# A mixture of experts in plain fp32 on parts of the matmul array, with one of three programs per expert chosen by its token count

## The chip, the core and the metric

The kernel runs on one core of a Trainium2 chip. A core has a matmul engine (PE; its weight loads are a row of their own, PEld), two engines for elementwise work (DVE, ACT), a general one (POOL) and a sequencer that issues most transfers here (SP). PE multiplies a stationary operand, which is loaded into its 128 by 128 array first (up to 128 rows, the contraction, by up to 128 columns, which become output partitions), with a moving operand that streams through. A matmul whose stationary operand has 64 or 32 columns takes a half or a quarter of the array's columns; it writes 64 or 32 of the 128 partitions of a PSUM bank (128 partitions by 512 fp32 numbers). Weights come from HBM through 16 transfer (DMA) engines. The metric is device time in microseconds (us), lower is better.

## What is computed

Two blocks over 256 tokens of width 1024. Each has a mixer (pooling, convolution, an RWKV recurrence) and a feed-forward part; the first block's is dense, the second's a mixture of eight experts of which each token takes two. The change is in that mixture:

```python
def moe_swiglu(h, router, w_gate, w_up, w_down):
    logits = (xf @ router)
    top_val, top_idx = lax.top_k(logits, TOP_K)          # TOP_K = 2
    gates = jax.nn.softmax(top_val, axis=-1)
    ...                                                   # tokens sorted by expert
    # for each expert e, on its own tokens x:
    #   y = (silu(x @ w_gate[e]) * (x @ w_up[e])) @ w_down[e]
    # and y, times the token's gate, is added to the token's row
```

A weight matrix has 1024 by 3584 numbers, three to an expert, eight experts: 352 MB in fp32, each read once. How many of the 512 token places each expert gets depends on the inputs. Evaluating the reference's routing on its inputs gives, for experts 0 to 7: 58, 77, 58, 62, 58, 73, 50, 76.

## The kernel before

The program is written out in the order in which each engine runs it. Mixer and dense part of the first block, then the mixer of the second, take the first 528 us or so; then come the routing (`route`, `pick`, `places`, `gates`: rank the logits, number the tokens of each expert) and the experts (`run_experts`).

An expert is worked off in 7 chunks of 512 hidden columns. For a chunk, `gate_up` multiplies the expert's tokens (up to 128 of them, gathered by a matmul with a one-hot matrix `ge` into `mx`, transposed, so that the tokens are the stationary columns) with 1024 by 512 numbers of the gate and as many of the up weights; ACT takes silu of the first product, DVE multiplies by the second (`msl`); `hidden` transposes that by four PE transposes (`mtp`); `down`, one chunk behind, multiplies it with 512 by 1024 numbers of the down weights and accumulates in two PSUM banks (`ya`) over the seven chunks. After an expert, `evac` takes `ya` out, scaled by the gates, and `scatter` puts the rows back to their tokens by a matmul with `gT` and adds them to the residual `h`.

All of these products are made from two parts of each operand. ACT rounds a weight to the shorter fp32r format (`wh`), DVE takes the rest (`wl`), the activations are split likewise (`mx`, `mhhl` hold both parts), and each product is three matmuls, high by high, high by low, low by high:

```python
mm(pg[a], xh[:, k, :], wh[:, kk, :], k == 0, False)
mm(pg[a], xh[:, k, :], wl[:, kk, :], False, False)
mm(pg[a], xl[:, k, :], wh[:, kk, :], False, k == KT - 1)
```

Weights come in units of 1 MB (128 partitions by 2048 numbers), six units to a chunk. `stream` holds 15 raw units; a unit's buffer is free again as soon as ACT and DVE have split it (three pairs of split buffers). If an expert had more than 128 tokens, a second pass under `tc.If(rv > P)` at the end would take the rest; the register `rv` is loaded from the greatest count there, on all engines, and the branch jumps over the second pass. After it, `finish` norms `h` and writes it out.

Of the kernel before, what the change touches and what calls it, by code (L numbers as in the profile page):

```python
# [18 lines left out]
P = 128  # L19
# [16 lines left out]
def kernel(  # L36
# [56 lines left out]
    def mm(o, lhsT, rhs, start, stop):  # L93
        nc.tensor.matmul(o, lhsT, rhs, start=start, stop=stop)  # L94

# [351 lines left out]
    def mixer(l, N, pend, nxt, open_next):  # L447
# [32 lines left out]
        v_ = vfirst if l == 0 else kp.tile([P, 4, T], F32, name=f"v{l}")  # L480
# [705 lines left out]

        return nxw, lambda q, halves=(0, 1): add_h(q, [wo[q, n] for n in range(2)], halves), tidy
# [118 lines left out]
    def route(R, hT, cmp, rt, ones, tie):  # L1306
# [55 lines left out]
        def count():  # L1362
            cps = mm_bank("cps")
            for q in range(2):
                mm(cps[:, :NE], ones, sel[:, q, :], q == 0, q == 1)
            cnt = small("cnt", [P, 1])
            vec.tensor_reduce(cnt, cps[:, :NE], axis=AX.X, op=OP.max)
            vec.tensor_copy(small("cnti", [P, 1], I32), cnt)

        return tr, logits, pick, places, gates, count  # L1370
# [4 lines left out]
    LAST = ((0, 512, 0, 2), (0, 512, 2, 4), (512, 768, 0, 4), (768, 1024, 0, 4))  # L1375
    FINE = 2
    HALVES = ((0, 512), (512, 1024))

    def expert_units():
        seq = [(e, c) for e in range(NE) for c in range(NCH)]  # L1380
        units = []

        def gate_up(e, c, nk=4):
            for nm, src in (("g", moe_w_gate[0, e]), ("u", moe_w_up[0, e])):
                for k in range(0, KT, nk):
                    units.append((src[k * P:(k + nk) * P, c * 512:(c + 1) * 512]
                                  .rearrange("(k p) n -> p k n", p=P), (nk, 512), f"m{nm}{e}{c}{k}"))

        def down(e, c, nj=2):
            for j in range(0, 4, nj):  # L1390
                r0 = c * 512 + j * P
                units.append((moe_w_down[0, e][r0:r0 + nj * P, :].rearrange("(k p) n -> p k n", p=P),
                              (nj, D), f"md{e}{c}{j}"))

        def last_down(e, c):
            for a, b, k0, k1 in LAST:
                r0 = c * 512
                units.append((moe_w_down[0, e][r0 + k0 * P:r0 + k1 * P, a:b].rearrange("(k p) n -> p k n", p=P),
                              (k1 - k0, b - a), f"ml{a}{k0}"))

        for i, s in enumerate(seq):
            fine = i >= len(seq) - FINE
            gate_up(*s, 2 if fine else 4)
            if i:
                down(*seq[i - 1], 1 if fine else 2)
        last_down(*seq[-1])
        return units

    def moe(W, R, pend, tidy, prep):
        rstd = R.rstd  # L1410
        st = ExitStack()
        mo = st.enter_context(tc.tile_pool(name="mo", bufs=1, reuse_waits="tile"))
        sx = st.enter_context(tc.tile_pool(name="sx", bufs=1, reuse_waits="tile"))
        m2 = st.enter_context(tc.tile_pool(name="m2", bufs=1, reuse_waits="tile"))
        spare = st.enter_context(tc.tile_pool(name="spare", bufs=1, reuse_waits="tile"))
        mx = [st.enter_context(tc.tile_pool(name=f"mx{i}", bufs=1, reuse_waits="tile")) for i in range(2)]
        sb, sa, sc = [st.enter_context(tc.tile_pool(name=f"s{i}", bufs=1, reuse_waits="tile")) for i in "bac"]
        W.pairs.extend(((sa, "h", sa, "l"), (sx, "h", sx, "l"), (sb, "h", sc, "l")))

        pend(0)  # L1420
        W.split(lambda *a: low(nc.gpsimd, *a, 0, 2048))
        low1, low2 = [], []
        W.split(lambda *a: low1.extend(a))
        low(vec, *low1, 0, 1024)
        W.after = lambda: (tidy(), W.open_raw(st, {"y": (m3, "big"), "x": (mx[1], "mx")}, (spare,)))
        m3 = st.enter_context(tc.tile_pool(name="m3", bufs=1, reuse_waits="tile"))
        hT = m3.tile([P, 2, KT, P], F32, name="hT", tag="big")
        tr, logits, pick, places, gates, count = route(R, hT, m2.tile([P, 2, T], F32, name="cmp", tag="msl"), *prep)
        hn = mo.tile([P, 2, D], F32, name="hn")

        def make_hn(q, half):
            ns = slice(half * 512, (half + 1) * 512)
            vec.scalar_tensor_tensor(hn[:, q, ns], h[:, q, ns], rstd[q], g2b[:, ns], op0=OP.mult, op1=OP.mult)

# [6 lines left out]
        W.split(lambda *a: low2.extend(a))  # L1441
# [4 lines left out]
        low(nc.gpsimd, *low2, 0, 2048)  # L1446
# [3 lines left out]
        pos = R.t["pos"]  # L1450

        def onehot(e, base):
            g = m2.tile([P, 2, P], F32, name="ge", tag="ge")
            for q in range(2):
                vec.tensor_scalar(g[:, q, :], iota_f, float(base), pos[:, q, e:e + 1], op0=OP.add, op1=OP.is_equal)
            return g

        def weigh(e, g):
            for q in range(2):
                vec.tensor_scalar(g[:, q, :], g[:, q, :], R.t["gate"][:, q, e:e + 1], None, op0=OP.mult)  # L1460
# [12 lines left out]
        def gather(e, g, idx, xh, xl, k4, between):  # L1473
# [5 lines left out]
            for f in between:  # L1479
                f()  # L1480
# [212 lines left out]
```

## Time and profile before

| | us |
|---|---|
| median of 3 runs (1569.64 to 1571.14) | 1570.03 |
| the profiled execution, its own time | 1567.63 |
| its span, first to last instruction | 1565.8 |
| first expert matmul to last (552.5 to 1549.3 in the trace) | 996.8 |

Times within the trace count from the span's start. An instruction's duration holds its way through the engine's pipeline, and matmuls overlap: what a matmul costs in a series is the distance from its start to the next one's, which a merged row of the timeline gives as its length less the last duration, over the count less one. One plain fp32 matmul of the program is two passes, so two records, each with its weight load; an fp32r matmul is one, and so is a transpose. "PEclk" is the granted share of PE's clock, 1.00 for 2.4 GHz and 0.50 for 1.2 GHz.

### The profile page before, as it was taken

The page shows a single profiled execution, that of the slowest core. Times are in us where ns is not written, and L with a number is a line of the kernel's source. Part 1 is how long each engine was busy: PE and PEld are TensorE (multiplying, and loading weights), DVE is VectorE, ACT ScalarE, POOL GpSimd, SP SyncE. Part 2 cuts the span into 40 slices and gives each one's busy share as a digit, 9 for nine tenths or more (in the row PEclk, how much of TensorE's full clock was granted, in tenths as well). Part 3 has the DMA queues.
Part 4 walks back from the last instruction along what each step waited for, and adds up shares of the span by engine and source line. Part 5 has one row for each costly group of instructions (what it writes and reads, how often), then busy time and mean ns, then how long its engine had stood idle before and what let it go on. Part 6 is the DMA issues. An engine that isn't in the chain of part 4 may idle for free. (4 is left out here: it accounts for less than half of the span.)

```text
span 1565.8 us, 25264 instructions
## 1 busy us (share of the span) xinstructions
PE 1519.3 (97%) x10388; PEld 1293.3 (83%) x10388; DVE 1279.8 (82%) x1381; ACT 976.6 (62%) x937; POOL 71.9 (5%) x90
## 2 busy tenths in 40 slices
PE   8999999999999899999999999999999999999996
PEld 7888899998988688888888888888888888888885
DVE  8997754556988778898888889889889889888986
ACT  6443644345533476776776777677677677677765
POOL 3201300000110300000000000000000000000000
PEclk9999999999999899999999999999999999999998
DMA  6416265524525688999999999999999999999872
GB/s 193 149 44 229 75 212 171 191 74 130 153 69 174 241 333 312 355 360 344 354 361 348 337 376 346 338 367 357 330 373 353 343 356 358 344 353 361 291 242 99
DMA packets 202965, 422.64 MB, mean 270 GB/s; under 512 B 8624, under 2 KB 53048, under 8 KB 202840
## 3 DMA queue, kind: packets, MB, share of 16 engines
q1 hardware_dynamic: 201880, 419.10, 75.5%
q8 instruction: 83, 1.36, 0.4%
q0 software_dynamic: 672, 1.31, 0.3%
q10 hardware_dynamic: 288, 0.52, 0.1%
q14 instruction: 42, 0.34, 0.1%
HBM read 419.86 MB, written 1.05 MB: 269 GB/s over the span
## 5 line engine op out<-in xcount | busy, mean ns | idle before, releaser
L148 DVE TENSOR_TENSOR wl_mu<-mu,wh_mu 128x2048 fp32r<-128x2048 f32 (+1 forms) x115 | 255.0, 2217 | 48.4 <-ACT wh_mu L144 47.6
L94 PE MATMUL m0a<-wh_mg,mx 128*128 128x512 f32 x896 | 294.1, 398 | 0.0
L94 PE MATMUL m1a<-wh_mu,mx 128*128 128x512 f32 x896 | 292.1, 395 | 0.0
L148 DVE TENSOR_TENSOR wl_md<-md,wh_md 128x2048 fp32r<-128x2048 f32 (+1 forms) x114 | 252.0, 2217 | 42.3 <-ACT wh_md L144 41.8
L94 PE MATMUL ya<-wh_md,mhhl 128*128 128x512 f32 x880 | 285.6, 395 | 0.0
L148 DVE TENSOR_TENSOR wl_mg<-mg,wh_mg 128x2048 fp32r<-128x2048 f32 (+1 forms) x114 | 251.8, 2215 | 21.2 <-ACT wh_mg L144 20.6
L144 ACT ACTIVATE wh_mg<-mg 128x2048 fp32r<-128x2048 f32 (+1 forms) x116 | 215.5, 1860 | 74.5 <-PE ya L94 41.6
L144 ACT ACTIVATE wh_md<-md 128x2048 fp32r<-128x2048 f32 (+1 forms) x114 | 211.9, 1858 | 64.1 <-PE m0a L94 32.8
L144 ACT ACTIVATE wh_mu<-mu 128x2048 fp32r<-128x2048 f32 (+1 forms) x116 | 215.2, 1855 | 23.0 <-PE m0a L94 21.9
L94 PEld LDWEIGHTS m1a<-wh_mu,mx 128*128 128x128 f32 x896 | 168.3, 188 | 36.9
L94 PEld LDWEIGHTS ya<-wh_md,mhhl 128*128 128x128 f32 x880 | 165.0, 187 | 40.0
L94 PEld LDWEIGHTS m0a<-wh_mg,mx 128*128 128x128 f32 x896 | 168.4, 188 | 35.6
L94 PE MATMUL m1a<-wl_mu,mx 128*128 128x512 f32 x448 | 175.9, 393 | 0.0
L94 PE MATMUL m0a<-wl_mg,mx 128*128 128x512 f32 x448 | 175.7, 392 | 0.0
L94 PE MATMUL ya<-wl_md,mhhl 128*128 128x512 f32 x440 | 173.9, 395 | 0.0
L94 PEld LDWEIGHTS ya<-wl_md,mhhl 128*128 128x128 f32 x440 | 82.5, 187 | 20.4 <-DVE wl_md L148 0.2
L94 PEld LDWEIGHTS m1a<-wl_mu,mx 128*128 128x128 f32 x448 | 84.2, 188 | 17.7
L94 PEld LDWEIGHTS m0a<-wl_mg,mx 128*128 128x128 f32 x448 | 84.3, 188 | 17.0 <-DVE wl_mg L148 0.6
L1528 ACT ACTIVATE mhhl<-mtpa 128x512 fp32r<-128x512 f32 x55 | 33.0, 600 | 71.8 <-PE mtpa L97 71.8
L94 PE MATMUL fps<-xhf,wl_fu 128*128 128x256 f32 x176 | 49.9, 284 | 0.0
L94 PE MATMUL fps<-xhf,wh_fg 128*128 128x256 f32 x176 | 49.9, 284 | 0.0
L94 PE MATMUL fps<-xhf,wh_fu 128*128 128x256 f32 x176 | 49.8, 283 | 0.0
(431 smaller groups left out, 2545.3 us busy)
## 6 DMA issues: line engine op xcount, KB each, us to landing
mg<-in_moe_w_gate_dram SPq DMA_DIRECT2D x108, 1024.0 KB
mu<-in_moe_w_up_dram SPq DMA_DIRECT2D x108, 1024.0 KB
md<-in_moe_w_down_dram SPq DMA_DIRECT2D x106, 1024.0 KB
fg<-in_ffn_w_gate_dram SPq DMA_DIRECT2D x11, 1024.0 KB
fu<-in_ffn_w_up_dram SPq DMA_DIRECT2D x11, 1024.0 KB
fd<-in_ffn_w_down_dram SPq DMA_DIRECT2D x11, 1024.0 KB
wo<-in_w_out_dram SPq DMA_DIRECT2D x16, 512.0 KB
wik<-in_w_in_dram SPq DMA_DIRECT2D x8, 512.0 KB
```

The source lines that it names most:

```text
L94: nc.tensor.matmul(o, lhsT, rhs, start=start, stop=stop)
L144: act(wh[:, :n], t[:, :n], AF.Copy)
L148: vec.tensor_tensor(wl[:, :n], t[:, :n], wh.bitcast(F32)[:, :n], op=OP.subtract)
L1528: act(hh, tp, AF.Copy)
```

## The change

The split is gone: weights and activations stay fp32, and PE multiplies them as they are. The tokens of an expert are laid out in up to three groups. The first 64 are the stationary operand of matmuls on a half of the array: in `half`, half `s` of the array takes 256 of the chunk's 512 weight columns, so that the two halves work on the same tokens and different columns. Tokens 64 to 95, and 96 to 127, are stationary on a quarter (32 columns), and the four quarters take 128 weight columns each. `down` does the same with 512 and 256 columns. Results of all groups share one bank: 256 columns of it for the first group, 128 for each of the others.

Each expert is written three times, with two, one or no group of 32 (`n`). From the counts, DVE works out a number 0, 1 or 2 per expert (more than 96 tokens, 65 to 96, up to 64); PE, ACT, DVE and SP load all eight numbers into registers and branch by them at each expert (`tc.Switch`), with a prefetch hint for the next expert in the fifth chunk. Of the counts above, experts 1, 5 and 7 run with `n` = 1 and the other five with `n` = 0.

The ring of raw units has 16 places (7 in space that the mixer gave up, as before, and 9 more); a unit's place is free when PE has used it. `scatter` multiplies out of fp32 too: it gives each token two one-hot rows (`gT`, five layers of it, weighted), and runs on 64 rows at a time. The counting is moved ahead of the experts. The closing of the program, the mixers and the dense part stay.

```diff
+    def mma(o, lhsT, rhs, start=False):
+        nc.tensor.matmul(o, lhsT, rhs, start=start, stop=True, skip_group_check=True)
...
+    class Feed:
...
+        def send(self):
+            if self.sent < len(self.units):
+                nc.sync.dma_start(self.view(self.sent), self.units[self.sent][0])
+                self.sent += 1
...
+    N_RAW = 9
...
+            vec.tensor_scalar(lev, cnt, 64.5, None, op0=OP.is_lt)
+            vec.scalar_tensor_tensor(lev, cnt, 96.5, lev, op0=OP.is_lt, op1=OP.add)
+            vec.tensor_copy(levi, lev)
...
+        def gather(e, b):
+            for k in range(KT):
+                for q in range(2):
+                    mm(AUX[:, 64 * k:64 * k + 64], hn[:, q, k * P:(k + 1) * P], ge[:, 0, q, 64 * b:64 * b + 64], q == 0, q == 1)
+            act(X[e % 2][:, :, 64 * b:64 * b + 64], AUX.rearrange("p (k t) -> p k t", k=KT), AF.Copy)
+
+        def half(o, x, us, n):
+            for k in range(KT):
+                for s in range(2):
+                    mma(o[64 * s:64 * s + 64, 0:256], x[:, k, 0:64], us[k // 4][:, k % 4, 256 * s:256 * s + 256], k == 0)
+            for k in range(KT):
+                for j in range(n):
+                    for t in range(4):
+                        mma(o[32 * t:32 * t + 32, 256 + P * j:256 + P * j + P],
+                            x[:, k, 64 + 32 * j:96 + 32 * j], us[k // 4][:, k % 4, P * t:P * t + P])
...
+        def down(c, us, n):
+            hT_ = Hid[c % 2]
+            for jj in range(4):
+                w = us[jj // 2][:, jj % 2, :]
+                o = (jj % 2) * P + (jj // 2) * 64
+                for s in range(2):
+                    mma(Y0[64 * s:64 * s + 64, :], hT_[:, o:o + 64], w[:, 512 * s:512 * s + 512], c == 0 and jj == 0)
...
+                    for t in range(4):
+                        mma(Y1[32 * t:32 * t + 32, 256 * j:256 * j + 256], hT_[:, o:o + 32], w[:, 256 * t:256 * t + 256],
+                            c == 0 and jj == 0 and j == 0)
...
+        def expert(e, n, base, hint):
...
+            if n:
+                gather(e, 1)
+            for c in range(NCH):
+                us = units(2)
+                half(GU[c % 2][0], x, us, n)
+                done(2)
+                if c:
+                    hidden(c - 1, n)
+                elif e:
+                    scatter(0)
+                us = units(2)
+                half(GU[c % 2][1], x, us, n)
+                done(2)
+                product(c, n)
+                if c:
+                    us = units(2)
+                    down(c - 1, us, n)
+                    done(2)
+                if c == 0 and e:
+                    scatter(1)
...
+                for e in range(NE):
+                    lv.append(nc.values_load(levi[0:1, e:e + 1], engines=ENG, min_val=0, max_val=2))
...
+                for arm in tc.Switch({g: lv[e] for g in ENG}, 3, hint=f"ex{e}" if e else None):
+                    W.used, W.sent = at
+                    expert(e, 2 - arm, base, hint)
```

PE's order in the middle of an expert before, from the last matmuls of one chunk's first product to the next product (`m0a` gate, `m1a` up, `mtpa` transposed hidden):

```order
L94 MATMUL m0a_6961<-wl_mg_6925,mx 128x512
L94 MATMUL m0a_6961<-wh_mg_6924,mx 128x512
L97 MATMUL mtpa_7049<-ident,msl 128x128 x4
L94 MATMUL m0a_6961<-wh_mg_6942,mx 128x512
L94 MATMUL m0a_6961<-wl_mg_6943,mx 128x512
L94 MATMUL m0a_6961<-wh_mg_6942,mx 128x512 x2
```

The transposes of the chunk before stand between two units of the gate product. And now on PE, in the middle of the first expert's program for up to 64 tokens, then at its exit, where the listing goes on with the next expert's jump and its first program (`mb` are the banks of gate and up, `mc` those of the transposes, the gather, and the down product, `ring` the raw units, `xT` and `mh` the tokens and the hidden values):

```order
L97 MATMUL mb_6908<-ring_6343,xT_6904 64x256 x8
L100 MATMUL mc_6910<-ident,sl_6900 128x128 x2
L97 MATMUL mb_6909<-ring_6422,xT_6904 64x256 x8
L97 MATMUL mb_6909<-ring_6424,xT_6904 64x256 x8
L97 MATMUL mc_6912<-ring_6426,mh_6902 64x512 x4
L97 MATMUL mc_6912<-ring_6428,mh_6902 64x512 x4
...
L1734 UNCONDITIONAL_BRANCH
L1734 SWITCH_STRIDE
L1734 ISA x2
L1655 BRANCH_PREFETCH_HINT
L94 MATMUL mc_6911<-ge,hn 128x64 x16
```

A chunk's 72 matmuls on the full array are 40 on halves (and 80 more on quarters where `n` is 1), the split parts `wh` and `wl` are no longer among the operands, and the transposes stand between the gate and the up product.

On DVE, between the last steps of the routing and the first expert, this stood before (`hn` the normed tokens, `ge` the one-hot matrix, `mx` the gathered tokens' low part):

```order
L1347 TENSOR_TENSOR pos<-pos,pps 128x16
L1455 TENSOR_SCALAR ge<-iota_f,pos 128x128 x2
L1433 SCALAR_TENSOR_TENSOR hn<-h,rstdm_6765,vfirst 128x512
L1433 SCALAR_TENSOR_TENSOR hn<-h,rstdm_6819,vfirst 128x512
L1351 TENSOR_REDUCE mx_6861<-lg 128x2
```

The one-hot matrix came right behind the tokens' numbers. On DVE this stands there now (`cnt`, `lev` the counts and the programs' numbers, `gT` and `ys` the operands of the scatter):

```order
L1351 TENSOR_TENSOR pos<-pos,pps 128x16
L1480 COPY cnt<-cps 128x8
L1481 TENSOR_SCALAR lev<-cnt 128x8
...
L1364 TENSOR_TENSOR gate<-ex,zs 128x16
L1499 MEMSET gT 128x1280
L1500 MEMSET ys 128x1024
L1505 TENSOR_SCALAR ge<-slot,pos 128x128 x8
L1644 TENSOR_LOAD levi x8
L1734 SWITCH_STRIDE
```

The one-hot matrix, which the first gather waits for, moves behind the counting, the gates and two memsets; eight register loads and the first branch follow.

## Rows read from the trace of the kernel before

**Rows 1.** The page's first two parts: busy time of each engine (share of the span, count), then the span in 40 slices, in tenths, and what the transfer engines moved.

```profile
PE 1519.3 (97%) x10388; PEld 1293.3 (83%) x10388; DVE 1279.8 (82%) x1381; ACT 976.6 (62%) x937; POOL 71.9 (5%) x90
PE   8999999999999899999999999999999999999996
PEclk9999999999999899999999999999999999999998
DMA  6416265524525688999999999999999999999872
```

**Rows 2.** The timeline of PE over one chunk: start, length, line, what is written and read, sizes, count.

```profile
903.31 0.60 PE L97 MATMUL mtpa<-ident,msl 128*128 128x128 f32 x4
903.66 0.48 PE L94 MATMUL m0a<-wh_mg,mx 128*128 128x512 f32 x1
...
909.26 0.39 PE L94 MATMUL m1a<-wh_mu,mx 128*128 128x512 f32 x1
...
914.79 0.39 PE L94 MATMUL ya<-wh_md,mhhl 128*128 128x512 f32 x1
...
920.74 0.48 PE L94 MATMUL m0a<-wh_mg,mx 128*128 128x512 f32 x1
```

**Rows 3.** Windows: length, busy time and count of PE, PEld, DVE, ACT, POOL, granted clock, share of the 16 transfer engines, GB/s. The experts as a whole, then 30 us at their start and two later, then a stretch of the mixer and one of the routing.

```profile
552.50:1549.30 996.80, 996.80 (x4567) 816.26 (x4567) 868.68 (x558) 714.91 (x506) 0.00 (x0) 1.00 0.94 340
560.00:590.00 30.00, 30.00 (x137) 24.52 (x136) 26.57 (x17) 22.85 (x17) 0.00 (x0) 1.00 1.04 394
860.00:890.00 30.00, 30.00 (x144) 24.68 (x143) 25.30 (x16) 21.10 (x16) 0.00 (x0) 1.00 0.89 329
1010.00:1040.00 30.00, 30.00 (x136) 24.46 (x135) 25.59 (x15) 21.86 (x15) 0.00 (x0) 1.00 1.00 370
80.00:100.00 20.00, 17.27 (x389) 16.32 (x386) 17.77 (x50) 7.07 (x16) 0.00 (x0) 1.00 0.17 55
540.00:550.00 10.00, 5.46 (x25) 5.30 (x26) 7.34 (x16) 1.66 (x3) 3.98 (x1) 0.50 0.34 105
```

**Rows 4.** The costliest groups of the page on DVE and ACT: busy time and mean duration, idle time before them and what ended it.

```profile
L148 DVE TENSOR_TENSOR wl_mu<-mu,wh_mu 128x2048 fp32r<-128x2048 f32 (+1 forms) x115 | 255.0, 2217 | 48.4 <-ACT wh_mu L144 47.6
L144 ACT ACTIVATE wh_mg<-mg 128x2048 fp32r<-128x2048 f32 (+1 forms) x116 | 215.5, 1860 | 74.5 <-PE ya L94 41.6
```

**Rows 5.** The timeline of PE in the mixers, where plain fp32 matmuls run on parts of the array: `vt` on halves in turn (128 rows by 64 columns), `y` on four parts of 64 by 64 (two groups of rows, two of columns), `st` on halves and then `wo` on the full array, `zz` in a long series on two parts.

```profile
106.98 1.97 PE L94 MATMUL vt<-ident,vfirst 128*64 128x128 f32 x32
...
134.83 1.62 PE L995 MATMUL st<-UV,BT 128*64 128x64 f32 x48
136.38 0.50 PE L94 MATMUL wo<-wh_wo,yh 128*128 128x512 f32 x1
136.72 0.40 PE L94 MATMUL wo<-wl_wo,yh 128*128 128x512 f32 x1
136.95 0.40 PE L94 MATMUL wo<-wh_wo,yl 128*128 128x512 f32 x1
...
146.38 1.15 PE L995 MATMUL y<-S,QT 64*64 64x64 f32 x48
...
469.80 1.98 PE L94 MATMUL zz<-Z,W 64*64 64x64 f32 x62
```

**Rows 6.** The same of plain fp32 on the full array, 256 columns moving, and the gather of the first expert, with the matmuls behind it.

```profile
160.60 0.60 PE L94 MATMUL g2ps<-xg,g 128*128 128x256 f32 x2
...
546.59 5.75 PE L94 MATMUL gaa<-ge,hn 128*128 128x128 f32 x32 [0.77 <-DVE ge L1455]
```

**Rows 7.** The timelines of DVE and POOL in the routing.

```profile
530.16 3.29 DVE L100 TENSOR_TENSOR wl_mg<-mg,wh_mg 128x1024 fp32r<-128x1024 f32 x1
...
540.84 3.22 DVE L1333 TENSOR_TENSOR cmp<-lg 128x64 f32<-128x64 f32 x1
543.98 0.21 DVE L1334 TENSOR_TENSOR cmp<-lg 128x64 f32<-128x64 f32 x1
...
546.16 0.48 DVE L1455 TENSOR_SCALAR ge<-iota_f,pos 128x128 f32<-128x128 f32 x2
546.55 1.41 DVE L1433 SCALAR_TENSOR_TENSOR hn<-h,rstdm,vfirst 128x512 f32<-128x512 f32 x2
...
550.15 0.17 DVE L1356 TENSOR_TENSOR ex<-ex,sel 128x16 f32<-128x16 f32 x1 [1.90 <-ACT ex L1355]
...
539.48 4.49 POOL L100 TENSOR_TENSOR wl_mu<-mu,wh_mu 128x2048 fp32r<-128x2048 f32 x1
```

**Rows 8.** The instructions of lines 1623 and 1624, the register load and the branch over the second pass: count, duration in ns (least, median, greatest), start.

```profile
L1623 PEldq TENSOR_LOAD <-cnti x1: 488/488/488, 1550.9 to 1550.9; - x1
...
L1623 SPq FUSED_REGOPS  x1: 177/177/177, 1530.8 to 1530.8; - x1
...
L1624 PEldq COMPARE_BRANCH  x1: 3775/3775/3775, 1551.5 to 1551.5; - x1
```

**Rows 9.** The timeline of all engines at the end.

```profile
1549.40 0.69 ACT L1556 ACTIVATE myhl<-ya,gs 128x512 fp32r<-128x512 f32 x1 [2.16 <-PE ya L94]
...
1550.79 2.47 DVE L1566 TENSOR_TENSOR h<-h,sca 128x512 f32<-128x512 f32 x4
...
1554.16 0.19 ACT L1633 ACTIVATION_READ_ACCUMULATOR junkza<-h 128x1 f32 x1
1555.78 0.69 DVE L1643 TENSOR_TENSOR o<-h,vfirst 128x512 f32<-128x512 f32 x1 [2.52 <-DVEq L1624]
```

More of the change, by code (lines that the diff above doesn't have):

```diff
@@ L1360, in gates @@
             vec.tensor_tensor(small("gate"), ex, zs[:, :, None].to_broadcast(S3), op=OP.mult)
[L1362 to L1370, printed above, removed]
+        return tr, logits, pick, places, gates
@@ new lines, in moe @@
+        count()
+        for q in range(2):
+            make_hn(q, 1)
+        gates()
+        ge = m2.tile([P, 4, 2, P], F32, name="ge")
+        gT = m2.tile([P, 5, T], F32, name="gT")
+        ys = kp.tile([P, 2, 512], F32, name="ys", tag="v")
+        SL = [m2.tile([P, 512], F32, name="sl0"), cvp.tile([P, 512], F32, name="sl1", tag="cva")]
+        Hid = [m2.tile([P, 512], F32, name=f"mh{i}") for i in range(2)]
+        X = [cr.tile([P, KT, P], F32, name=f"xT{i}", tag=("TT", "VQ")[i]) for i in range(2)]
@@ new lines, in expert, with units, done @@
+        def expert(e, n, base, hint):
+            x = X[e % 2]
+            def units(k):
+                return W.get(k)
+            def done(k):
+                for _ in range(k):
+                    W.send()
+            if n:
+                gather(e, 1)
+            for c in range(NCH):
+                us = units(2)
[9 more added lines that the diff above has]
+                product(c, n)
+                if c:
+                    us = units(2)
[3 more added lines that the diff above has]
+                    scatter(1)
+                if c == 1:
+                    weigh(e)
+                if c == 2:
+                    scatter_ops(0)
+                if c == 3:
+                    if n == 2:
+                        scatter_ops(1)
+                    if e + 1 < NE:
+                        onehot(e + 1, base)
+                if c == 4:
+                    hint()
+            hidden(NCH - 1, n)
+            if e + 1 < NE:
+                gather(e + 1, 0)
+            us = units(2)
+            down(NCH - 1, us, n)
+            done(2)
+            evac(n)
@@ L1611, in run_experts @@
-            for part in LAST[0:3]:
-                products(*part)
-            evac(e, HALVES[0:1])
-            products(*LAST[3])
-            evac(e, HALVES[1:2])
-            for n in range(2):
-                junk = acc_bank(f"junkz{idx}{n}")
-                for q in range(2):
-                    scatter(e, q, HALVES[n:n + 1])
-                    closing(q, n, junk)
-        run_experts(0, "a", W.get, [lambda: [make_hn(q, 1) for q in range(2)], gates, lambda: low(vec, *low1, 1024, 2048)])
@@ L1623, in moe @@
-        rv = nc.values_load(R.t["cnti"][0:1, 0:1], min_val=0, max_val=T)
+            for q in range(2):
+                scatter(q)
+                for n in range(2):
+                    closing(q, n, GU[q][n])
+        run_experts(0)
+        rv = nc.values_load(cmaxi[0:1, 0:1], min_val=0, max_val=T)
         with tc.If(rv > P):
-            W.feed(expert_units())
-            run_experts(P, "b", W.get, [])
+            W.units.extend(expert_units())
+            for _ in W.ring:
+                W.send()
+            run_experts(P)
@@ L1627, in moe @@
         st.close()
+        tidy()
     ssz = cst.tile([P, 2, 2], F32, name="ssz")
```

301 lines of the change are left out of this document (123 added, 178 removed).

## Prediction

> **What bounds the kernel now.** First the slices: from 552 us on PE is busy in every slice, at full clock, and the transfer engines too [rows 1]. Two candidates, then, and the busy shares can't part them. So I read one chunk in PE's timeline: gate product at 903.66, next chunk's gate product at 920.74, 17.08 us, with matmuls about 0.23 us apart and no idle note [rows 2]. 72 matmuls of 512 columns and 4 transposes fill it: PE sets the pace. Then the windows: over the experts 340 GB/s arrive, but in 560 to 590, just after the ring was emptied and buffers came free fast, 394 [rows 3]; later windows (329, 370) are lower because PE and the split free buffers no faster. At 394 GB/s a unit of 1.049 MB takes 2.66 us and a chunk's six 16.0 us, only 1.1 us less than PE's 17.08. Transfers are the second bound, close behind. DVE and ACT are busy 869 and 715 us of 997, nearly all with the split [rows 3, 4], and wait for each other and for PE.
>
> So taking work off PE, DVE and ACT can pay at most until transfers bound: 336 units by 2.66 us are 894 us, 43 us of it ahead of the experts (16 units). The question is what PE needs now.
>
> **The matmuls, passes first.** A plain fp32 matmul is two passes. A pass of 256 columns on the full array costs 0.60 − 0.38 = 0.22 us (0.38 is the length of one such pass, and of the row's two the second starts 0.22 after the first) [rows 6]; I take 0.216. On halves in turn, `vt` runs 32 passes of 128 columns in 1.97 us; less the last one's 0.27 that is 1.70 over 31, 0.055 us per pass. One pass of 128 columns by itself takes half of 0.22, 0.11: so two halves do run at once, and a pair of passes costs one [rows 5]. The extents of `half` are twice these, which can only help against fixed costs.
>
> Quarters are not in the trace. Four parts at once are: `y`, on two row groups by two column groups, runs 48 passes in 1.15 − 0.22 = 0.93 us, 0.020 each, where 64 columns take 0.055 alone: 2.8 at a time on average [rows 5]. Bounds for a quarter pass of 128 columns, by the nearest rows: 0.11/4 = 0.027 if four run at once, 0.055 if only two do as in `vt`. PE issues fast enough for the first: `zz`, 62 passes in 1.98 − 0.22, is 0.029 per pass with its weight load. I take 0.027, nearer to `y`, the only row with four parts, and keep 0.055.
>
> The Trainium skill says otherwise (TensorE: Matmul & The Clock Gate, Part 3, What overlaps and what doesn't): matmuls start strictly in order, and a weight load goes beside a running matmul only if the row groups differ. Both speak against this change, since all its parts share all rows and the two passes of one matmul stand one behind the other. By the first, quarters run two at a time and the sum below is 1604; by the second, halves wouldn't overlap. `vt` has all rows in both halves and overlaps, and 0.020 in `y` is less than the 0.029 that starting in order would allow, so the trace bears out neither.
>
> **A chunk.** Gate and up on halves: 2 × 16 pairs × 0.216 = 6.9 us. Down: 8 pairs of 512 columns, twice 0.216 each, 3.45. Two transposes, 0.11 each (4 in 0.60, less 0.27, over 3) [rows 2]. Going over from one division of the array to another: `st` to `wo` shows 0.1 us until `wo` starts and 0.1 more until its second matmul is in step (0.34 behind the first, then 0.23) [rows 5]; 0.2 each, twice a chunk with `n` = 0. Sum 11.0 us. With `n` = 1 add 2 × 64 quarter passes × 0.027 = 3.5, 32 of 256 columns at 0.054 = 1.7, a transpose and five more changes, 1.1: 17.3 us (with 0.055: 5.2 more, 22.5).
>
> **Around an expert.** The wait for the hidden values of the last chunk 0.5 and the gather for the next: 32 passes of 64 columns, each with a load of 128, 0.11 each plus ACT's copy, 3.9 (twice with `n` = 1); two scatters, each 4 passes of 512 on two row groups at once and 16 of 256, 2.8 each, and a change each, 6.4 in all; `gT` transposes 0.8. The branch: the jump over the second pass held PE 3.78 us [rows 8]. Each expert has two jumps, out of the program and into the next; the hint names the second. Bounds 0.1 and 7.6; I take 6, as one fetch and some of another, beside full transfer queues. That makes 77 + 17.6 = 94 us for `n` = 0, 82 for expert 0 (no scatter, no branch), 121 + 21.5 = 142 for experts 1 and 5, 138 for 7 (no gather behind it).
>
> **Before the experts.** Gone are the splits between the routing steps: DVE's 3.29 us and the 3.22 us of a compare that takes 0.23 elsewhere and runs beside POOL's split [rows 7]; some 4 us of it on the path to the numbers. Added ahead of the first gather: counting 1.2 us, `hn`'s second half 1.4, the gates with the wait for ACT 3.0, two memsets about 2, eight compares instead of two about 1.5 (0.24 each), 9 in all; of the gather, 6.8 us at the low clock (5.75 for a run that ends at the high one [rows 6]) instead of that, and then register loads, 8 × (0.49 + 0.18) = 5.4, partly beside the gather, and the first branch, without hint, 3.8. I put the first expert matmul at 562 instead of 552.5 and 3 us more for its cold clock (0.50 in this stretch [rows 3]). The sixteen units are there by then.
>
> **The sum.** Transfers: 42 units an expert, 112 us at 2.66. Expert 0 takes 82 us from a full ring; 1 takes 142, in which the ring fills. Experts 2, 3 and 4 need 126 units; I count 10 of the 16 as there at the start, since the pair in use and those in flight aren't, and 116 × 2.66 = 309 us is more than 3 × 94, so transfers bound these. Expert 5: 142. Expert 6 from a full ring: 94. Expert 7: 138. Sum 907. From 565 that is 1472. Behind it evacuation 1.1, two scatters with DVE's adds between (2.47 for four [rows 9]) 8, the squares 1; from 1554.2 to the end of the span 11.6 stay as they were [rows 9], less 1 to 2 beside other work: 20. Span 1492; the profiled execution was 1.8 over its span, and 2.4 under the median of the runs, so 1496. ACT and DVE are covered: per chunk a silu and a multiplication of 0.7 at most, a copy as long, under 11 us. With their split gone, what is late next is PE or the ring. SP issues behind PE's release of a unit, 16 units ahead, so its own branch delays nothing.
>
> The Trainium skill gives a core's share of HBM as about 358 GB/s (DMA: Bandwidth & Descriptors, Specifications); by that a unit takes 2.93 us and the sum becomes an estimated 1550. The 394 over 30 us [rows 3] says more is to be had.
>
> **Rivals.** (1) Quarters two at a time: 21 chunks by 5.2 us, 109 us less what waiting for transfers gives back (nothing: experts 1, 5 and 7 are bound by PE): 1604, slower. For it: no row has four column groups; against: `y`. It decides from 0.045 us per quarter pass (74 us of gain over 21 chunks is 3.5 us each). (2) Boundaries dearer: PE idle over the branches drops to the low clock, as it was in the routing (0.50, PE busy half of the time [rows 3]), and both fetches stand in full: 12 to 14 us an expert, in the five that PE bounds: 1535. For it, the 3.78 of the branch; against, the mixers, where PE kept 1.00 through many small waits [rows 3]. (3) PE never the bound: quarters and changes cheaper than counted, transfers run through: 565 + (336 − 16) × 2.66 + some 25 = 1441. (4) PE falls to the low clock while it waits for transfers, or halves don't overlap at these lengths: a chunk of 20 us or more in every expert, over 1700. Against the first: waits would be under 2 us between bursts of 3.5; against the second, `vt`. (5) The branch takes dearer programs than the counts say (`n` = 2 everywhere): 7 more chunks' worth each, over 1750; against: the thresholds are in the diff, and the counts have no value near 64.5 or 96.5.
>
> **Chances.** Forecast, 1460 to 1535 with all small costs moved: 0.52. Rival 1: 0.13, and quarters in between, about 1540 to 1565: 0.07. Rival 2: 0.13. Rival 3: 0.08. Rivals 4 and 5: 0.07. The range 1450 to 1590 leaves out most of rivals 1, 3, 4 and 5. Faster than before by over 0.2% (3 us, what this measurement can tell from none): forecast, rivals 2 and 3 and the in-between, 0.80; slower 0.18 (rivals 1, 4, 5, less a little); the same 0.02.
>
> **What would show it.** Passes of `mb` in pairs 0.22 us apart, and 32 by 128 in fours 0.11 apart; chunks of 11.0 and 17.3 us; PE waiting for transfers in experts 3 and 4 alone; a rate near 394 GB/s there, lower in 1, 5 and 7; 4 to 8 us without matmuls between experts; first expert matmul at 562. It is wrong if quarters come in twos, if the clock row falls under 1.00 inside experts, or if the rate where PE waits is under 380.

## The result, and the profile after

The changed kernel takes 1504.86 us, median of 4 runs (1503.98 to 1509.16), against 1570.59 for the kernel before in the same series; ratio 0.9587, 95% interval 0.9568 to 0.9606. Faster, as forecast, and 9 us over the 1496. The profiled execution took 1505.09, its span 1503.3.

The page's busy times and slices, against [rows 1]:

```profile
PE 1376.8 (92%) x14461; PEld 981.4 (65%) x14461; DVE 498.8 (33%) x1066; ACT 300.8 (20%) x529; POOL 61.8 (4%) x88
PE   7999999999999969979997979879779997979996
PEclk9999999999999969979998999989979999999999
DMA  6415345541532659999997999999999997999940
GB/s 187 153 58 193 121 160 190 188 141 57 167 103 71 240 225 368 406 401 401 382 342 272 404 402 404 407 405 405 407 400 400 392 380 258 404 404 398 372 177 31
```

DVE and ACT have become nearly idle among the experts, with the split gone. Two things are new: PE has dents (7) at the boundaries between experts and its clock (7 and 8) at four of the seven, and the transfers run at 400 GB/s in most slices, where they had 330 to 370.

PE's timeline at the start, then a chunk with `n` = 0 (`mb` gate and up products, `mc` transposes and down product), the boundary of experts 0 and 1, and a chunk with `n` = 1; columns as in [rows 2]:

```profile
561.59 11.96 PE L97 MATMUL mb<-ring,xT 128*64 128x256 f32 x96 [3.37 <-issue]
...
606.80 0.44 PE L100 MATMUL mc<-ident,sl 128*128 128x128 f32 x2
607.16 3.67 PE L97 MATMUL mb<-ring,xT 128*64 128x256 f32 x32
610.67 3.60 PE L97 MATMUL mc<-ring,mh 128*64 128x512 f32 x16
614.10 3.62 PE L97 MATMUL mb<-ring,xT 128*64 128x256 f32 x32
617.65 0.44 PE L100 MATMUL mc<-ident,sl 128*128 128x128 f32 x2
...
639.81 3.65 PE L97 MATMUL mc<-ring,mh 128*64 128x512 f32 x16
651.61 7.06 PE L94 MATMUL mc<-ge,hn 128*128 128x64 f32 x32 [8.15 <-issue]
658.60 7.92 PE L97 MATMUL mb<-ring,xT 128*64 128x256 f32 x96
...
745.71 5.56 PE L97 MATMUL mb<-ring,xT 128*64 128x256 f32 x96
751.19 0.55 PE L100 MATMUL mc<-ident,sl 128*128 128x128 f32 x3
751.67 5.56 PE L97 MATMUL mb<-ring,xT 128*64 128x256 f32 x96
757.16 5.52 PE L97 MATMUL mc<-ring,mh 128*64 128x512 f32 x48
762.61 5.56 PE L97 MATMUL mb<-ring,xT 128*64 128x256 f32 x96
```

The first expert matmul comes at 561.59. A chunk is 617.65 − 606.80 = 10.85 us with `n` = 0 and 762.61 − 745.71 = 16.90 with `n` = 1. A merged row names one form only; the 96 of `mb` are 32 passes on halves and 64 on quarters, 5.48 us from start to start against 3.56 for the 32 alone (603.24 to 606.80 in the same timeline), so 0.030 us a quarter pass, the change from halves included. The boundary shows 8.15 us without a matmul, and the gather behind it takes 7.06 us; the same gather ahead of it took 3.68 (636.19).

What PE waited for from 562 to 1484 (total, times, longest):

```profile
PE mb L97 <- issue: 36.6, 5, 8.7
PE mc L94 <- issue: 25.1, 3, 8.8
PE mb L97 <- DMA ring<-in_moe_w_gate_dram: 4.3, 6, 0.9
PE mc L97 <- DMA ring<-in_moe_w_down_dram: 3.9, 7, 0.7
PE mb L97 <- DMA ring<-in_moe_w_up_dram: 3.7, 8, 0.7
```

"issue" is the branches: 61.7 us with the first, so 58.3 for the seven boundaries between experts. Transfers cost 11.9 us openly. Windows, one per expert (0 to 7; the last ends ahead of its last down product), columns as in [rows 3]:

```profile
561.59:643.46 81.87, 81.87 (x610) 46.19 (x610) 8.75 (x25) 5.68 (x12) 0.00 (x0) 0.98 0.98 378
643.46:789.03 145.57, 137.42 (x1810) 86.39 (x1809) 12.97 (x29) 6.93 (x14) 0.00 (x0) 0.94 1.01 381
789.03:886.68 97.65, 89.29 (x650) 50.20 (x650) 11.32 (x29) 4.77 (x12) 0.00 (x0) 0.95 0.94 353
886.68:990.52 103.84, 89.92 (x651) 49.21 (x650) 11.32 (x29) 4.99 (x12) 0.00 (x0) 0.97 1.04 404
990.52:1099.83 109.31, 92.42 (x651) 49.63 (x650) 11.32 (x29) 4.99 (x12) 0.00 (x0) 0.95 1.04 405
1099.83:1246.20 146.37, 137.62 (x1809) 86.49 (x1809) 12.97 (x29) 6.93 (x14) 0.00 (x0) 0.94 1.01 386
1246.20:1342.07 95.87, 87.91 (x651) 49.44 (x650) 11.32 (x29) 4.77 (x12) 0.00 (x0) 0.96 0.95 359
1342.07:1478.20 136.13, 127.32 (x1731) 80.28 (x1731) 11.19 (x21) 5.74 (x12) 0.00 (x0) 0.95 0.78 294
```

Experts 2, 3 and 4 have the same work and take 97.7, 103.8 and 109.3 us: 3 and 4 are the two in which the transfers run without a break, at 404 and 405 GB/s.

### The profile page after: what moved, and what is told of

Same layout as the page of the kernel before. It is cut to its first block, busy times and chain, and to the rows that moved or that the text cites. A ratio compares the mean times of both kernels' runs of the same rounds, so it can differ in the third digit from the quotient of the medians.

```text
span 1503.3 us, 32581 instructions
## 1 busy us (share of the span) xinstructions
PE 1376.8 (92%) x14461; PEld 981.4 (65%) x14461; DVE 498.8 (33%) x1066; ACT 300.8 (20%) x529; POOL 61.8 (4%) x88
## 5 line engine op out<-in xcount | busy, mean ns | idle before, releaser
L97 PE MATMUL mb<-ring,xT 128*32 128x128 f32 (+1 forms) x6272 | 507.8, 342 | 44.7 <-issue 36.6
L97 PEld LDWEIGHTS mb<-ring,xT 128*32 128x32 f32 (+1 forms) x6272 | 329.7, 128 | 217.8 <-issue 100.5
L97 PE MATMUL mc<-ring,mh 128*64 128x512 f32 (+1 forms) x1568 | 243.6, 504 | 6.5 <-DMA ring<-in_moe_w_down_dram 3.9
L97 PEld LDWEIGHTS mc<-ring,mh 128*64 128x64 f32 (+1 forms) x1568 | 81.3, 125 | 141.5 <-issue 112.8
L94 PE MATMUL mc<-ge,hn 128*128 128x64 f32 x352 | 54.1, 327 | 33.0 <-issue 25.1
L94 PEld LDWEIGHTS mc<-ge,hn 128*128 128x128 f32 x352 | 53.2, 243 | 35.6 <-issue 27.6
L94 PE MATMUL fps<-xlf,wh_fu 128*128 128x256 f32 x176 | 49.8, 283 | 0.0
L94 PE MATMUL fps<-xlf,wh_fg 128*128 128x256 f32 x176 | 49.8, 283 | 0.0
L94 PE MATMUL fps<-xhf,wl_fg 128*128 128x256 f32 x176 | 49.8, 283 | 0.0
L557 DVE SCALAR_TENSOR_TENSOR cy<-cu,parC,cy 128x256 f32<-128x256 f32 x120 | 49.6, 476 | 0.0
```

Of the source, the lines that this page charges most:

```text
L97: nc.tensor.matmul(o, lhsT, rhs, start=start, stop=True, skip_group_check=True)
L557: vec.scalar_tensor_tensor(cy[:, i, :], src, wc, cy[:, i, :], op0=OP.mult, op1=OP.add)
```

## The experiments

**The branches.** First the question what the boundaries are worth. `e_line` writes every expert once, with the program that these counts ask for; it serves these counts only.

```diff
-                    lv.append(nc.values_load(levi[0:1, e:e + 1], engines=ENG, min_val=0, max_val=2))
+                lv = [0, 1, 0, 0, 0, 1, 0, 1]
-                for arm in tc.Switch({g: lv[e] for g in ENG}, 3, hint=f"ex{e}" if e else None):
-                    W.used, W.sent = at
-                    expert(e, 2 - arm, base, hint)
+                expert(e, lv[e], base, lambda: None)
```

> The branches are taken out: every expert is written once, straight on, with the program that its count asks for (n = 0, 1, 0, 0, 0, 1, 0, 1), without register loads. All arithmetic stays. Boundary theory (what stands between 1505 us and the transfers' floor are the seven boundaries, 8.2 us without matmuls and 2 to 6 us of low clock behind each): experts 1, 5, 6 and 7 lose 14, 15, 10 and 13 us, experts 2 to 4 together only 10, since they become bound by transfers; 1440 to 1450 us, and no low clock inside the experts. Transfer theory (the transfers run at 369 of 405 GB/s over the experts already and hide the boundaries): not under 1480 us.

Measured: 1447.53 us (1446.50 to 1448.57), ratio to the kernel before 0.9218 (0.9202 to 0.9233), where the boundary theory said 1440 to 1450. Its boundary of experts 0 and 1 in PE's timeline, and one window over the experts:

```profile
636.32 3.65 PE L97 MATMUL mc<-ring,mh 128*64 128x512 f32 x16
639.91 3.79 PE L94 MATMUL mc<-ge,hn 128*128 128x64 f32 x32
643.62 5.56 PE L97 MATMUL mb<-ring,xT 128*64 128x256 f32 x96
```

```profile
560.00:1400.00 840.00, 804.05 (x8269) 465.73 (x8269) 89.54 (x216) 43.11 (x98) 0.00 (x0) 1.00 1.04 401
```

No pause, the gather 3.79 instead of 7.06, the first gate product 5.56 instead of 7.92: at this boundary the pause cost 8.15 us and the low clock behind it 5.6. The low clock costs least where no second gather stands behind the boundary: at expert 3 the first 32 passes took 5.40 us (895.40) instead of 3.67. Not all of it comes back. 58.3 us of pauses, some 26 of low clock (the stretches at 0.50 behind the seven boundaries hold some 52 us of matmuls, at half speed) and 4.9 at the start (first expert matmul at 556.69) are 89, but the span fell by 58.6. The rest went to the transfers: over 840 us they run at 401 GB/s, and PE's waits for units rose from 11.9 to 32.5 us. The profile counts a wait only from the end of the last matmul's row; from one start to the next, the gaps of 0.6 to 3 us, which leaves out the pauses at the boundaries, rose from 18 to 48 us. The waits in `e_line`:

```profile
PE mb L97 <- DMA ring<-in_moe_w_up_dram: 12.0, 22, 1.5
PE mb L97 <- DMA ring<-in_moe_w_gate_dram: 10.6, 17, 0.9
PE mc L97 <- DMA ring<-in_moe_w_down_dram: 9.9, 17, 0.8
```

So the boundaries are what kept the kernel off the transfers' floor, and behind them that floor comes soon.

**The hint.** `e_nohint` leaves out every prefetch hint; `e_latehint` puts it behind the last transposes of an expert, ahead of the next gather.

```diff
-                if c == 4:
-                    hint()
...
+            hint()
             if e + 1 < NE:
                 gather(e + 1, 0)
```

(The added line stands in `e_latehint` alone.)

> The branches stay, the prefetch hints go. If the hint shortens the jump into an expert, PE's jump grows from 5.3 to 5.6 us by at least 1 us, and the time by 3 to 20 us. If it does nothing: the same jumps, within 3 us of 1505. If it does harm: the jump is 3.3 us as at the first expert, which has no hint in front of its branch, and the time is 8 to 15 us lower.

> The hint moves from the fifth chunk to the place in front of the gather for the next expert, the last thing but one before the branch. If an early hint is lost because the engine goes on to fetch its own straight-on instructions, a late one works: PE's jump under 1 us, the stretch without matmuls 3 us instead of 8.2, 1470 to 1485 us. If the hint does nothing wherever it stands: jumps of 5.3 us and within 3 us of 1505.

Measured: 1502.20 us without (1500.13 to 1502.61; ratio 0.9543 to 0.9575) and 1501.13 late (1498.64 to 1502.12; 0.9539 to 0.9571). Both intervals reach into that of the changed kernel: a hint gives nothing that can be told here, wherever it stands. PE's branches at a boundary (count, least, median and greatest duration in ns, first and last start), of the changed kernel behind experts 0 and 1, then without hints behind expert 2:

```profile
L1734 PEldq COMPARE_BRANCH  x2: 5284/5590/5895, 639.8 to 646.1; - x2
L1734 PEldq COMPARE_BRANCH  x2: 3573/4583/5593, 787.6 to 791.5; - x2
```

```profile
L1732 PEldq COMPARE_BRANCH  x2: 4154/5797/7440, 877.3 to 881.8; - x2
```

The first of the two is the exit of a program, the second the jump into the next; here 5.90 and 5.28 us, 3.57 and 5.59, 4.15 and 7.44. The pause is what of both the last matmuls don't cover: 3.6 us are covered behind a program with `n` = 0, whose exit starts that long before its last matmul ends, and 1.5 behind one with `n` = 1. Without hints the jumps are longer (7.0 to 7.4 us where 5.3 to 5.6 stood) and the exits shorter (1.7 to 4.3 us, and one of 0.32, where 3.4 to 6.2 stood), and the pauses stay, 7.8 to 8.7 us at six of the seven boundaries. The seventh, behind the exit of 0.32, is 4.36. With the late hint the jumps are 5.1 to 5.8 us and the pauses 8.1 to 8.7, but for one of 2.64 behind an exit of 0.45. Why these two exits cost next to nothing stays open. My three theories on the hint all fell: it shortens the one and doesn't move the sum.

**Why a branch is slow.** The first jump of the changed kernel, with no hint and hardly any transfers running, took 3.3 us; the later ones over 5. `e_nodma` leaves out the weight transfers behind the first sixteen units.

```diff
-            if self.sent < len(self.units):
+            if self.sent < 16:
```

> Left out: all weight transfers after the first sixteen units, so that all experts multiply by the numbers that lie in the ring. PE never waits for a unit and nothing moves beside the branches' own fetches. If the fetches of a branch are slow because they stand in line with weights: PE's jump into an expert 3.3 us as at the first expert instead of 5.4, the stretch without matmuls 5 to 6 us, in all 1460 to 1475 us. If weights don't matter to them: 5.4 and 8.2 us as before, in all 1505 less the 20 us in which PE waited for units, 1482 to 1488.

Measured: 1451.19 us in a single run, below both numbers. PE's two branches at the boundary of experts 0 and 1, its timeline there, and the window around it; then, of the changed kernel, the same window and one over the exit of expert 1:

```profile
L1734 PEldq COMPARE_BRANCH  x2: 2704/3026/3349, 640.7 to 644.4; - x2
```

```profile
640.70 3.65 PE L97 MATMUL mc<-ring,mh 128*64 128x512 f32 x16
647.38 5.04 PE L94 MATMUL mc<-ge,hn 128*128 128x64 f32 x26 [3.03 <-issue]
```

```profile
641.00:652.00 11.00, 7.97 (x42) 5.51 (x38) 0.00 (x0) 1.00 (x2) 0.00 (x0) 0.83 0.02 6
```

```profile
641.00:652.00 11.00, 2.85 (x14) 1.00 (x11) 0.00 (x0) 0.60 (x1) 0.00 (x0) 0.74 1.05 403
787.57:791.14 3.57, 1.46 (x28) 0.63 (x20) 0.00 (x0) 0.68 (x2) 0.00 (x0) 1.00 0.53 148
```

With 6 GB/s instead of 403 moving, the exit takes 3.35 us instead of 5.90, the jump 2.70 instead of 5.28, and the pause is 3.03 instead of 8.15. Over the seven boundaries it is 3.0 to 3.8 behind a program with `n` = 0 and 5.6 to 6.0 behind one with `n` = 1, 28.2 in all instead of 58.3. The changed kernel by itself shows the same: its exits behind experts 1 and 5, with 148 and 135 GB/s moving, took 3.6 and 3.4 us, the other five, with 380 to 403, took 5.9 to 6.2.

What the branches wait for is in the trace too, as instruction transfers among the DMA queues. Over the two branches (639.8 to 651.4 in the changed kernel, with the weights' queue above it, and 640.7 to 647.2 in `e_nodma`: packets, MB, share of 16 engines):

```profile
q1 hardware_dynamic: 2316, 4.61, 103.5%
q8 instruction: 2, 0.03, 1.0%
```

```profile
q8 instruction: 2, 0.03, 1.8%
```

Each of these branches has one packet of 16 KB on that queue. In both runs it takes 0.88 to 0.95 us, and the branch ends 1.4 to 1.5 us behind it. But it starts 1.0 us into the exit and 0.3 into the jump in `e_nodma`, and 3.5 and 2.9 us into them in the changed kernel; the exits of 0.32 and 0.45 us above have no such packet. So the fetch itself is no slower beside weights; it starts later. The theory of the line is right, and I had undervalued it: some 30 us of the 58. Of the 54 us gained, 18 more are the waits for units, counted from start to start as above, and some 6 are less time at the low clock.

**Order and overlap on the array.** The forecast rests on halves and quarters running at once. `e_series` takes the same matmuls half by half and quarter by quarter, `e_blocks` the halves in blocks of two matmuls (four passes).

```diff
-            for k in range(KT):
-                for s in range(2):
+            for s in range(2):
+                for k in range(KT):
...
-                for j in range(n):
-                    for t in range(4):
+            for j in range(n):
+                for t in range(4):
+                    for k in range(KT):
```

```diff
+            for s, k in [(s, b + i) for b in range(0, KT, 2) for s in range(2) for i in range(2)]:
```

> Gate and up products in another order: all eight matmuls of one half of the array, then all of the other, and the same for the quarters (all on the first quarter, then the second, ...). Same work. If parts overlap only when neighbours in the order lie on different parts: the gate and up part of a chunk with n = 0 doubles, 6.9 to 13.8 us, a chunk 17.8; with n = 1 the quarters cost 128 x (0.11 - 0.026) = 10.8 us more on top, a chunk 34.7; in all 2050 to 2130 us. If each part has its own queue, the order doesn't matter: 1505.

> The matmuls of the first group go in blocks of two, so four passes on one half, then four on the other, where they alternated by matmul. If PE starts a few matmuls ahead of one that waits for its half (as the order half by half suggested, where gate took 5.8 us and not 6.9): a chunk with n = 0 at most 11.5 us. If matmuls start strictly in their order: three of four passes stand alone, 8 x 3 x 0.216 = 5.2 us per product instead of 3.45, a chunk of 14.3 us.

Measured: 1930.11 us for `e_series`, a single run; a chunk with `n` = 0 is 1012.17 − 996.83 = 15.34 us, between 10.85 and the 17.8 of strict turns, and a product with `n` = 1 goes from 5.5 to 12.1 us. For `e_blocks` 1511.39 us, a single run too, and a chunk of 609.40 − 598.50 = 10.90. PE's timeline in `e_series`:

```profile
996.83 5.67 PE L97 MATMUL mb<-ring,xT 128*64 128x256 f32 x29
1002.12 0.64 PE L97 MATMUL mc<-ring,mh 128*64 128x512 f32 x1
1002.33 0.59 PE L97 MATMUL mb<-ring,xT 128*64 128x256 f32 x2
1002.60 0.59 PE L97 MATMUL mc<-ring,mh 128*64 128x512 f32 x1
...
1012.17 5.67 PE L97 MATMUL mb<-ring,xT 128*64 128x256 f32 x29
```

The gain is indeed from parts side by side: without neighbours on the other half 4.5 us a chunk are lost, of the 7 that strict turns would cost. But starts are not strictly in the program's order. At 1002.12 the down product's first pass, on the first half, starts while three passes of the up product, which stand ahead of it in the program and belong to the second half, have not started. So PE let a pass for a free half go ahead of three that waited for theirs; four passes in a block cost nothing measurable, sixteen do.

**Fewer branches.** `e_pair` puts two experts into a program, with five programs for their two counts and a number that DVE works out from both; it serves any counts, as the changed kernel does.

```diff
+            vec.tensor_tensor(low, pr[:, :, 0], pr[:, :, 1], op=OP.min)
+            vec.tensor_scalar(low, low, 1.0, None, op0=OP.min)
+            vec.scalar_tensor_tensor(pair, pr[:, :, 0], 2.0, pr[:, :, 1], op0=OP.mult, op1=OP.add)
+            vec.scalar_tensor_tensor(pair, pair, -2.0, low, op0=OP.add, op1=OP.mult)
...
+                for arm in tc.Switch({g: lv[e // 2] for g in ENG}, 5, hint=None):
+                    W.used, W.sent = at
+                    for i, n in enumerate(((2, 2), (1, 1), (1, 0), (0, 1), (0, 0))[arm]):
+                        expert(e + i, n, base, lambda: None)
```

> Two experts to a program and five programs (both with n = 2, or n = 1 and 1, 1 and 0, 0 and 1, 0 and 0), branched to by a number that DVE works out from two counts, without hints; four branches instead of eight, four register loads instead of eight. Boundary theory: the boundaries ahead of experts 1, 3, 5 and 7 go; 1 gives back 14 us, 5 gives 15, 7 gives 13, 3 nearly nothing by itself since experts 2 to 4 are then bound by transfers, 10 for the three; and the start 2 us: 1450 to 1460. If the larger programs make each of the three boundaries left longer, they show stretches over 9 us without matmuls and the time is over 1465.

Measured: 1477.45 us (1476.81 to 1478.58), ratio 0.9406 (0.9390 to 0.9421). Better than the changed kernel, but short of the boundary theory's 1450 to 1460. The boundaries that are left show pauses of 12.2, 4.8 and 6.8 us, so the other theory's sign, over 9 us, holds for one of three. Part of the loss is the rate: 394 GB/s in a stretch in which PE waits for units, where the changed kernel has 404. Two runs asked whether the size of the program does this, one by two more programs per expert that no count asks for, one with three programs per pair instead of five:

```diff
-                for arm in tc.Switch({g: lv[e] for g in ENG}, 3, hint=f"ex{e}" if e else None):
+                for arm in tc.Switch({g: lv[e] for g in ENG}, 5, hint=f"ex{e}" if e else None):
-                    expert(e, 2 - arm, base, hint)
+                    expert(e, max(0, 2 - arm), base, hint)
```

```diff
+            vec.scalar_tensor_tensor(pair, pr[:, :, 0], 1.5, pr[:, :, 1], op0=OP.is_ge, op1=OP.mult)
...
+                    for i, n in enumerate(((2, 2), (0, 1), (0, 0))[arm]):
```

> The changed kernel with two more programs per expert that no count asks for (40 programs in all, as many as the version with two experts to a program has, where 24 were). That version moved its weights at 393 GB/s where it waited for them, this kernel at 404. If the size of the program in memory lowers the rate: 393 GB/s where PE waits, experts 2 to 4 about 8 us longer, 1510 to 1518 us. If size doesn't matter: 404, and within 3 us of 1505.

> Two experts to a program, but three programs to a pair (n = 0 and 1, 0 and 0, and 2 and 2 for all else): 24 expert programs as in the changed kernel. If the size of the program lowered the rate in the version with five: 404 GB/s, and 320 units at 2.59 instead of 2.67 us, 1450 to 1458 us. If it is something else in the pairing: 393 and 1470 to 1478.

Measured: `e_fat` 1508.02 us in a single run. In windows of 10 us from 890 to 1100 it moves 386 to 416 GB/s where the changed kernel has 388 to 417, but for two dips, 358 at 910 and 313 at 1020, whose cause stays open. `e_pair3` takes 1475.64 us (1473.95 to 1476.95), with 394 and 395 GB/s where PE waits. Size is not what sets the rate.

**The place of the buffers.** What the two paired versions share is a few small tiles more, which stand ahead of the ring. In the changed kernel nine of the sixteen ring places begin at a multiple of 512 bytes within a partition; in `e_pair` and `e_pair3` these are 64 and 32 bytes off, and none does. Three runs move nothing but places: `e_mis` puts the nine off, `e_al` puts all sixteen on, `e_pair_al` does the latter in `e_pair`.

```diff
+    cst.tile([P, 8], F32, name="padl")
```

```diff
+    ctx.enter_context(tc.tile_pool(name="padr", bufs=1, side="right")).tile([P, 120], F32, name="padr")
```

(The first is `e_mis`, the second `e_al`; `e_pair_al` has the second, and the first with 112 numbers for 8.)

> The changed kernel with 32 bytes per partition reserved ahead of the ring, nothing else. In the changed kernel nine of the sixteen ring places begin at a multiple of 512 bytes in a partition and seven do not; in both versions with two experts to a program the new small tiles had moved the nine off it by 64 or 32 bytes. If the place of the buffers sets the rate: 394 GB/s instead of 404 where PE waits, 126 units x 0.07 us = 8 us more over experts 2 to 4, 1510 to 1516 us. If not: 404 and 1505 within 3.

> The changed kernel with 480 bytes per partition reserved at the other end, so that all sixteen ring places begin at a multiple of 512 bytes. If the place sets the rate, with 88 ns per 2 KB piece off it (the versions with two experts) and 85.4 on the mean of nine on and seven off: 83.3 ns with all on, some 414 GB/s where PE waits, 1496 to 1500 us. If not: 404 and 1505.

> Two experts to a program, five programs, with the tiles so placed that all sixteen ring places begin at a multiple of 512 bytes. If the place set the 393 GB/s of that version: over 404 where PE waits, and 1448 to 1458 us, near the 1447 of the version without branches. If the pairing itself did: 393 and 1475 to 1480.

Measured: `e_mis` 1513.95 us (1512.63 to 1515.36; ratio 0.9616 to 0.9648, outside the changed kernel's), `e_al` 1503.15 (1499.04 to 1506.38; 0.9542 to 0.9587), `e_pair_al` 1466.18 (1463.12 to 1468.37; 0.9312 to 0.9346). The same 40 us of `e_mis`, of the changed kernel and of `e_al`, the last column the rate:

```profile
900.00:940.00 40.00, 40.00 (x312) 23.05 (x312) 6.42 (x15) 2.65 (x7) 0.00 (x0) 1.00 1.04 393
```

```profile
900.00:940.00 40.00, 40.00 (x316) 23.17 (x314) 5.89 (x12) 2.64 (x7) 0.00 (x0) 1.00 1.04 404
```

```profile
900.00:940.00 40.00, 40.00 (x316) 23.19 (x314) 5.89 (x12) 2.65 (x7) 0.00 (x0) 1.00 1.04 410
```

None, nine and sixteen places on the multiple: 393, 404 and 410 GB/s, and `e_pair` went from 394 to 413 in 910 to 970. For the changed kernel the step from nine to sixteen can't be told in its time, since only two experts wait for transfers; the step down to none cost 9 us; for the paired version, which waits in more of them, all sixteen are worth 11. The changed kernel's own trace shows the places side by side: between 890 and 1095 us a piece of 2 KB took 87.3 ns on average into the seven places off the multiple and 84.4 into the nine on it (pieces told apart by the order of their starts). In `e_mis` it took 88.3 into both groups, in `e_al` 84.3. The Trainium skill (DMA: Bandwidth & Descriptors, How a descriptor splits into AXI transactions) says of what a transfer reads that, where it doesn't start at a multiple of 256 bytes, its first access begins at the boundary below and fetches bytes that go unused. That is the same direction, but here it is the written side that moved, of which that section gives no such rule; and these runs can't tell 256 from 512.

`e_pair_al` beats both kernels, the one before by 6.7% and the changed one by 2.6% (1466.18 against 1504.86). It stays above the 1448 to 1458 that I expected: its boundaries still show 11.8, 5.1 and 6.7 us and a low clock behind them, and PE waits 18.2 us for units.

## Why the prediction was right, step by step

**Before the experts**: first expert matmul at 562, measured 561.59. The 3 us for its cold clock were too many: the first 96 passes took 11.89 us from start to start, three products of 3.5 and 1.4 more.

**A chunk**: 11.0 and 17.3 forecast, 10.85 and 16.90 measured. Halves cost one pass per pair, and quarters 0.030 with their change, so rival 1 (0.055) is out; it would have shown a product of 7 us instead of 5.5. `y` in [rows 5] was the right row to go by. The Trainium skill's rule of strictly ordered starts (TensorE: Matmul & The Clock Gate, Part 3, What overlaps and what doesn't), by which the sum would have been 1604, does not hold here: `e_series` shows starts ahead of their turn, and `e_blocks` loses nothing.

**Around an expert**: this is the step that failed. "I take 6, as one fetch and some of another" stands against pauses of 8.0 to 8.8 us, 58.3 over seven, and behind each 2 to 6 us of low clock, some 26 in all, which I had counted for the first expert only: 12 for 6. Both fetches stand: exit and jump took 8.8 to 11.8 us together at each boundary, less the 1.5 or 3.6 beside the last matmuls. A sign that I had named for being wrong was met, too: the clock row did fall under 1.00 inside the experts (0.94 to 0.97 from expert 1 on). The price of 3.78 came from the branch in [rows 8], which ran at the kernel's end with no weights moving; `e_nodma` shows that without weights the pauses are indeed 3.0 to 6.0. "Beside full transfer queues" stood in the text without a price of its own. Rival 2 had the mechanism, both fetches in full and the low clock behind them, and nearly the price: 12 to 14 us per expert against 9.5 to 14.7 in those that PE bounds. Its time, 1535, was wrong since it kept all else as forecast.

**What made up for it**: the work of an expert beside its boundary was less than counted, 145.6 − 8.2 − 5.6 = 131.8 us for expert 1 where 136 stood (142 without the branch), and a unit took 2.59 us at 404 GB/s, not 2.66. By experts: 82 for 85 (cold clock included), 146 for 142, 311 for 309 (2 to 4), 146 for 142, 96 for 94, and 142 for 138 (1342.07 to 1483.7). These are 922 for 910, and with 0.4 less each at the start and the end the span comes out at 1503 instead of 1492. That 1496 came so near is partly luck. In experts 1, 5, 6 and 7, which PE bounds, the boundaries cost 27 us more than counted and the work 13 us less; in 2 to 4 the transfers set the time, which covered most of what the boundaries there cost above the 6. And the 2.4 us between the profiled execution and the median, which I had carried over, did not come again (1505.09 and 1504.86).

**Transfers**: bound in experts 3 and 4, as forecast, with the ring covering expert 2; 309 us for the three, measured 310.8. `e_line` adds that rival 3 (transfers run through, 1441) is nearly what is left when the branches go, at 1447.5. The Trainium skill's 358 GB/s (DMA: Bandwidth & Descriptors, Specifications), an estimated 1550, is half of what two cores share, and on this one core it is not borne out: 404 to 413.

**The end**: 20 us from the last down product, measured 1503.3 − 1483.7 = 19.6.

**SP**: its own branch delays nothing, I wrote. In the changed kernel's trace SP's sixteen branches took 43 to 82 ns each, so they cost nothing by themselves; no run took them apart from the others.

## What to carry to other kernels

Price a branch in the traffic in which it will run: the same kind of jump cost 3 us on a quiet chip and over 5 beside a full stream of weights, and the engine's clock fell behind it, so that a boundary cost 12 us, and three of them instead of seven (`e_pair_al` against `e_al`, 37 us) were worth more than any hint. Where transfers bound, look at where the buffers lie: moving small tiles alone shifted the rate between 393 and 410 GB/s, and it hid in an unrelated edit. And check a sum that comes out right by its terms.

## What the runs showed that I had not expected

- The rate of transfers depends on where their buffers begin: 393, 404 and 410 GB/s with none, nine and sixteen of sixteen on a multiple of 512 bytes. The 394 of [rows 3], on which I built the unit's 2.66 us, is near the first of these, and a 2 KB piece took 88.2 ns in that stretch, as in `e_mis`; whether for the same reason was not tried.
- PE starts matmuls ahead of their turn when their half of the array is free: blocks of four passes cost nothing (10.90 us a chunk), blocks of sixteen 4.5 us a chunk.
- A prefetch hint shortened PE's jumps from over 7 to 5.5 us and left all pauses but one as they were. Why the exits took the difference back stays open.
- Behind a program with `n` = 1 the pause is 5.6 to 6.0 us even with no weights moving, behind `n` = 0 3.0 to 3.8. The branches take about as long behind both (exits of 3.3 to 3.8 us, jumps of 2.7 to 3.1); what differs is how much of the exit the last matmuls cover, 1.5 us or 3.6.
